# Mamba-2 part of a trunk kernel: channels on partitions, the group norm one stage later, the first output projections behind the last group's z columns

## The chip, the cores and the metric

The kernel runs on one core of a Trainium2 chip. The metric is the device time of one execution in microseconds: 1997.97 as the median of three (1996.41 to 1998.56). Profiles show one execution each. TensorE (PE) multiplies, VectorE (DVE), ScalarE (ACT) and GpSimd (POOL) do the rest, SyncE (SP) and POOL issue the DMAs. Each engine works through its own list in order; semaphores join the lists.

## What is computed

One layer of a decoder trunk on x of shape (1, 1024, 1024): a layer norm, a wide projection, a Conformer convolution branch beside a Mamba-2 branch, gates, an output projection, a second norm, a convolutional feed-forward block and a last norm. The change lies in the Mamba-2 branch (32 heads of 64 channels, four groups, state of 128, chunks of 128 positions):

```python
h = layer_norm(x, ln_in_g, ln_in_b)
u_glu, z, xbc, dt_raw, gate_a, gate_b = split_in(h @ w_in)
# in ssd_branch:
xbc = silu(causal_dwconv(xbc, conv_w, conv_b))           # xs, bm, cm
dt = softplus(dt_raw + dt_bias);  a = dt * -exp(a_log)
# in ssd_chunked, per chunk:
a_cs = cumsum(a)
y_diag = einsum("bcgrls,bcsgrp->bclgrp", cb * decay, xs * dt)
y_off  = einsum("bclgn,bcgrpn,bcgrl->bclgrp", cc, prev, exp(a_cs))
y = y_diag + y_off + xh * d_skip
yg = y * silu(z)                                          # groups of 512 channels
yg = yg * rsqrt(mean(square(yg), axis=-1) + RMS_EPS)      # per group and position
y_b = (yg * norm_w) @ w_ssm_out
mix = (sigmoid(gate_a) * y_a + sigmoid(gate_b) * y_b) @ w_o
```

## The kernel before

The 1024 positions go in two halves of 512 (`hh`). Activations stand channel-major in hT (128 channels on partitions, 512 positions along). fp32 products are made of three fp32r matmuls (`mm3`, L183 to L185: high by high, low by high, high by low); `project` (L187) makes one *column*, 128 output channels by 512 positions, of 24 matmuls 128x512. Its weights come by a DMA on SP, and `weights` splits them into high and low parts (cast on ACT L159, subtraction on DVE L160). Columns accumulate in four PSUM banks ("acc", `bank(1)`), everything else in four others ("sm", `bank(0)`).

`mixers` runs, per half, a stage for each of the four SSD groups: two columns for B and C (w_c), four for x, four for the gate z (`z_gate`, L478), two pairs for the Conformer part (`glu`: ga and gg), then `ssd_group` (L499) with its four chunks. Behind the groups come eight columns gt; then `combine` alternates gate columns (gb) with the second halves of the SSM output projection (sp). The first halves (so, `ssm_out_first`, which needs the normed groups 0 and 1) stand behind the SSD part of group 2. The 31-tap convolution (`conv31`, L467 on DVE) is recorded at low priority and fills VectorE's gaps.

In the SSD part positions stand on partitions. Per chunk, x is transposed (px), m = decay times CB is made, L562 computes po = C S (one matmul of 512 columns), L581 py (8 heads, m stationary, 64 columns of xs moving). VectorE puts t together: skip term (L551), yo (L564), t+yo (L567), t+py (L582), t times zs (L583); ACT squares it with a row sum into ssq (L585). zs comes from `z_gate` with positions on partitions as well. It has five buffers, and L583 is the last reader of each. `normed` then takes the root of four columns of ssq (L588, L589), scales the four t (L591) and transposes them into yT (16 transposes, L209, split into two parts at L215 and L216), where `so` and `sp` read them.

The order on each engine is fixed when the program is built: a simulated timeline chooses among ready instructions by priority. The pools' buffers decide who waits for whom.

Of the kernel before, what the change touches and what calls it, by code (L numbers as in the profile page):

```python
# [8 lines left out]
F32 = mybir.dt.float32  # L9
# [36 lines left out]
RW_NW = 6 * D  # L46
RW_AL = RW_NW + 2 * D
RW_SD = RW_AL + HEADS
RW_N = RW_SD + HEADS

# [6 lines left out]
def kernel(  # L57
# [71 lines left out]
    dskip = statep.tile([P, HEADS], F32, name="dskip")  # L129
# [8 lines left out]
    edc = statep.tile([P, 3, 4, HEADS], F32, name="edc")  # L138
# [12 lines left out]
    g_scr = [dram.tile([8, P, HALF], F32, name=f"g_scr{i}") for i in range(2)]  # L151
    y_scr = [dram.tile([8, P, HALF], F32, name=f"y_scr{i}") for i in range(2)]
# [111 lines left out]
    def ln_in(hh):  # L264
        hT = big_tile(f"hT{hh}")
        with pool(f"lnin{hh}", side="right") as pl:
# [12 lines left out]
            if first:  # L279
                SY.dma_start(pc[:, :PC_N], pcol)  # L280
                SY.dma_start(a_log, prow[RW_AL : RW_AL + HEADS].partition_broadcast(P))
                SY.dma_start(dskip, prow[RW_SD : RW_SD + HEADS].partition_broadcast(P))
# [12 lines left out]
    def time_steps(pl, hh, ps):  # L295

        n2 = 2 * HEADS
        dtc = pl.tile([n2, HALF], F32, tag="yo", name=f"dtc{hh}")
# [48 lines left out]
        for c in range(4):  # L347
# [6 lines left out]
            )  # L354
        hi = pl.tile([P, HALF], F32R, tag="xsd", name=f"sp_hi{hh}")
# [21 lines left out]
        A.activation(out=ev, in_=pe[:, : 3 * n], func=AF.Exp)  # L377
        V.tensor_mul(wds, dtv, edc[:, 1].rearrange("p c h -> p (c h)"))
# [99 lines left out]
    def z_gate(pl, hh, hT, g):  # L478

        pss = [bank(1) for _ in range(4)]  # L480
        for kp in range(4):
            w = weights(wz[g, kp], f"z{hh}_{g}_{kp}")
            for t in range(4):
                for k in range(2):
                    mm3(
                        pss[t],
                        lambda i: hT[:, i, 2 * kp + k, t * P : (t + 1) * P],
                        lambda i: w[:, i, k * HALF : (k + 1) * HALF],
                        kp == 0 and k == 0,
                        kp == 3 and k == 1,  # L490
                    )
        zs = []
        for t in range(4):
            z = pl.tile([P, HALF], F32, tag="zs", bufs=5, name=f"zs{hh}_{g}_{t}")
            A.activation(out=z, in_=pss[t], func=AF.Silu)
# [821 lines left out]
```

## Time and profile before

| | before |
|---|---|
| median of three runs | 1997.97 us |
| profiled execution | 1997.83 us, span 1995.9 us |
| mean granted TensorE clock | 0.998 |
| PE sum of matmuls L209 on t, L562, L581 | 15.3, 28.6, 60.5 us |
| DVE from 100 to 400 us | busy 298.40 of 300 us |
| DVE from 800 to 1050 us | busy 249.46 of 250 us |

The two stretches of VectorE are the mixers' group stages of the first and of the second half (TensorE is busy for 298.88 and 250.00 us in them). Busy times of overlapping matmuls are merged, and the mean of one record is its latency; what a stream of records costs is seen from the start of one to the start of the next.

### The profile page before, as it was taken

What the parts mean: (1) busy time and instruction counts of PE and PEld (TensorE: products, weight loads), DVE (VectorE), ACT (ScalarE), POOL (GpSimd) and SP (SyncE); (2) the same over time, 40 slices, a digit from 0 to 9 for tenths busy, and PEclk for the clock granted to TensorE, in tenths of its full rate; (3) what the DMA queues carried; (4) which work ended last, traced back from release to release, by engine and by line L of the source; (5) the groups of instructions that cost most, each with busy time, mean ns of one, the idle gap of its engine ahead of it and who ended that gap; (6) DMA issues with size and microseconds to landing.
All of it is one profiled execution on the core that took longest, in us unless ns stands there. A gap on an engine that the chain in (4) does not pass through costs nothing. (4 is left out here: it accounts for less than half of the span.)

```text
span 1995.9 us, 24560 instructions
## 1 busy us (share of the span) xinstructions
PE 1963.0 (98%) x9140; PEld 1619.0 (81%) x9140; DVE 1688.2 (85%) x2257; ACT 1025.6 (51%) x1490; POOL 170.2 (9%) x143
## 2 busy tenths in 40 slices
PE   7999999999999999999999999999999999999997
PEld 6888887888788888888888888887878888888886
DVE  7599999989865868999998987578998888788868
ACT  5465654556453265665545546255555544553432
POOL 1010101001310000100000122001000000011000
PEclk9999999999999999999999999999999999999999
DMA  6213223333445632222323243477443232368572
GB/s 223 95 64 96 80 89 107 96 111 102 168 136 164 229 124 74 85 90 85 116 90 111 101 166 125 137 277 250 154 155 110 100 122 95 106 225 270 181 242 106
DMA packets 97032, 272.21 MB, mean 136 GB/s; under 512 B 11216, under 2 KB 11216, under 8 KB 96912
## 3 DMA queue, kind: packets, MB, share of 16 engines
q1 hardware_dynamic: 88992, 246.78, 36.8%
q0 software_dynamic: 5616, 19.66, 2.7%
q10 hardware_dynamic: 2304, 4.20, 0.6%
q8 instruction: 72, 1.18, 0.2%
q14 instruction: 48, 0.39, 0.1%
HBM read 221.05 MB, written 49.55 MB: 136 GB/s over the span
## 5 line engine op out<-in xcount | busy, mean ns | idle before, releaser
L467 DVE SCALAR_TENSOR_TENSOR c<-v,pc,c 128x512 f32<-128x512 f32 x480 | 374.5, 803 | 7.1 <-ACT c L456 5.6
L525 POOL TENSOR_TENSOR au<-seg_mv,head_of 128x1024 fp32r<-128x1024 f32 x32 | 74.8, 2336 | 958.6 <-PE sm L534 728.7
L183 PE MATMUL acc<-hT,w_c 128*128 128x512 f32 x352 | 140.9, 400 | 0.0
L184 PE MATMUL acc<-hT,w_c 128*128 128x512 f32 x352 | 140.6, 399 | 0.0
L185 PE MATMUL acc<-hT,w_c 128*128 128x512 f32 x352 | 138.5, 394 | 0.0
L956 DVE SCALAR_TENSOR_TENSOR fo<-u,pc,fo 128x1024 f32<-128x1024 f32 x88 | 111.3, 1284 | 0.4 <-ACT fo L952 0.4
L422 DVE SCALAR_TENSOR_TENSOR xbc<-u,pc,xbc 128x512 f32<-128x512 f32 x144 | 109.6, 773 | 0.5 <-ACT xbc L420 0.4
L183 PE MATMUL acc<-h1s,w_s 128*128 128x512 f32 x264 | 103.4, 392 | 2.3 <-ACT u L940 2.3
L185 PE MATMUL acc<-h1s,w_s 128*128 128x512 f32 x264 | 103.0, 390 | 0.0
L184 PE MATMUL acc<-h1s,w_s 128*128 128x512 f32 x264 | 102.8, 389 | 0.0
L184 PE MATMUL acc<-w_z,hT 128*128 128x512 f32 x256 | 100.9, 394 | 0.0
L183 PE MATMUL acc<-w_z,hT 128*128 128x512 f32 x256 | 100.7, 400 | 0.0
L185 PE MATMUL acc<-w_z,hT 128*128 128x512 f32 x256 | 100.6, 396 | 0.0
L159 ACT CAST w_c<-st_c 128x1024 fp32r<-128x1024 f32 x48 | 50.4, 1051 | 91.8 <-PE acc L185 67.5
L1095 ACT CAST w_dn<-dr 128x1024 fp32r<-128x1024 f32 (+1 forms) x73 | 60.9, 843 | 67.9 <-DVE dr L1025 35.0
L1096 DVE TENSOR_TENSOR w_dn<-dr,w_dn 128x1024 fp32r<-128x1024 f32 (+1 forms) x73 | 70.2, 967 | 14.7 <-ACT w_dn L1095 14.5
L184 PEld LDWEIGHTS acc<-hT,w_c 128*128 128x128 f32 x352 | 66.1, 188 | 16.8 <-issue 3.9
L185 PEld LDWEIGHTS acc<-hT,w_c 128*128 128x128 f32 x352 | 66.1, 188 | 16.1 <-issue 2.6
L183 PEld LDWEIGHTS acc<-hT,w_c 128*128 128x128 f32 x352 | 66.1, 188 | 15.9 <-issue 2.6
L160 DVE TENSOR_TENSOR w_c<-st_c,w_c 128x1024 fp32r<-128x1024 f32 x46 | 59.3, 1288 | 16.7 <-ACT w_c L159 16.7
L183 PE MATMUL sm<-h1b,w_s 128*128 128x512 f32 x176 | 69.1, 393 | 0.0
L184 PE MATMUL sm<-h1b,w_s 128*128 128x512 f32 x176 | 69.0, 392 | 0.0
(366 smaller groups left out, 5698.0 us busy)
## 6 DMA issues: line engine op xcount, KB each, us to landing
st_c<-wcol SPq DMA_DIRECT2D x50, 512.0 KB, 3.5
st_z<-wz SPq DMA_DIRECT2D x32, 512.0 KB, 3.4
st_wo<-wo SPq DMA_DIRECT2D x24, 512.0 KB, 4.2
ra<-wup SPq DMA_DIRECT2D x22, 512.0 KB, 3.5
rb<-wup SPq DMA_DIRECT2D x22, 512.0 KB, 3.4
t_scr<-fo POOLq DMA_DIRECT2D x22, 512.0 KB, 3.4
dr<-t_scr SPq DMA_DIRECT2D x44, 256.0 KB, 4.0
dr<-wdown SPq DMA_DIRECT2D x38, 256.0 KB, 4.3
```

Of the source, the lines that this page charges most:

```text
L159: A.copy(w[:, 0, :], st)
L160: (eng or V).tensor_tensor(out=w[:, 1, :], in0=st, in1=w[:, 0, :].bitcast(F32), op=ALU.subtract)
L183: TE.matmul(ps, wa(0), xa(0), start=start, stop=False, skip_group_check=more)
L184: TE.matmul(ps, wa(0), xa(1), start=False, stop=False, skip_group_check=more)
L185: TE.matmul(ps, wa(1), xa(0), start=False, stop=stop, skip_group_check=more)
L422: V.scalar_tensor_tensor(out=o, in0=u[:, k : k + HALF], scalar=pc[:, wc + k : wc + k + 1], in1=o, op0=ALU.mult, op1=ALU.add,)
L467: V.scalar_tensor_tensor(out=accs[i], in0=v[:, k : k + HALF], scalar=pc[:, wc + k : wc + k + 1], in1=accs[i], op0=ALU.mult, op1=ALU.add,)
L525: G.tensor_tensor(out=au, in0=seg_mv[:, c, :].unsqueeze(1).to_broadcast([P, 8, P]), in1=head_of[:, g, :].unsqueeze(2).to_broadcast([P, 8, P]),
L956: V.scalar_tensor_tensor(out=o, in0=u[:, k : k + T], scalar=pc[:, wc + k : wc + k + 1], in1=o, op0=ALU.mult, op1=ALU.add,)
L1095: A.copy(w[:, 0, cs], src)
L1096: V.tensor_tensor(out=w[:, 1, cs], in0=src, in1=w[:, 0, cs].bitcast(F32), op=ALU.subtract)
```

## The change

z and y now stand with channels on partitions. `z_gate` makes four ordinary columns; one zs holds 128 channels by 512 positions. The exponentials of the cumulated decay, which scaled yo, are written to DRAM once per half (e_scr) and loaded by two broadcasting DMAs on POOL's queue into ys, which the group's four chunks then share (one buffer). A chunk multiplies its slice of ys by po (L564; po now four matmuls of 128 columns, L563) and adds py (L587; xs stationary with 64 columns, m moving with 128, heads alternately on the lower and the upper 64 partitions, L577). After the last chunk follow, per 128 channels, the skip term (L591), the multiplication by zs (L595), Square (L597, L600), and POOL sums the squares (L601). `normed` adds over partitions with four small matmuls (L606), takes the root (L611, L612), sends r to DRAM and back to all partitions (L614, L615), scales (L618) and splits (L203, L204). The transposes of t are gone, and the rows of norm_w too (nskip holds norm_w and D per channel). `done` of group g is called behind the z columns of group g+1, that of group 3 behind the second gt column; `ssm_out_first` behind the z columns of group 3.

```diff
-    dskip = statep.tile([P, HEADS], F32, name="dskip")
+    nskip = statep.tile([P, 2, 16], F32, name="nskip")
+    pick = statep.tile([P, 4, 4], F32, name="pick")
+    V.memset(pick, 0.0)
+    for c in range(4):
+        V.memset(pick[:, c, c : c + 1], 1.0)
...
+    e_scr = [dram.tile([P, HALF], F32, name=f"e_scr{i}") for i in range(2)]
+    r_scr = [dram.tile([GROUPS, HALF], F32, name=f"r_scr{i}") for i in range(2)]
...
+        eh = pl.tile([P, HALF], F32, tag="yo", bufs=2, name=f"sp_eh{hh}")
+        A.activation(out=eh, in_=pa, func=AF.Exp)
+        G.dma_start(e_scr[hh], eh)
...
-        for i, m in enumerate((upper, later, ones)):
+        for i, m in enumerate((later, ones)):
...
     def z_gate(pl, hh, hT, g):
 
-        pss = [bank(1) for _ in range(4)]
-        for kp in range(4):
-            w = weights(wz[g, kp], f"z{hh}_{g}_{kp}")
-            for t in range(4):
-                for k in range(2):
-                    mm3(
-                        pss[t],
-                        lambda i: hT[:, i, 2 * kp + k, t * P : (t + 1) * P],
-                        lambda i: w[:, i, k * HALF : (k + 1) * HALF],
-                        kp == 0 and k == 0,
-                        kp == 3 and k == 1,
-                    )
         zs = []
-        for t in range(4):
-            z = pl.tile([P, HALF], F32, tag="zs", bufs=5, name=f"zs{hh}_{g}_{t}")
-            A.activation(out=z, in_=pss[t], func=AF.Silu)
+        for i in range(4):
+            ps = bank(1)
+            project(ps, weights(wz[4 * g + i], f"z{hh}_{g}_{i}"), hT)
+            z = pl.tile([P, HALF], F32, tag="zs", bufs=5, name=f"zs{hh}_{g}_{i}")
+            A.activation(out=z, in_=ps, func=AF.Silu)
             zs.append(z)
         return zs
 
     def ssd_group(pl, hh, g, xT, BT, CT, zs):
         S = states[g]
         h8 = slice(8 * g, 8 * g + 8)
-        nw = row(pl, RW_NW + g * HALF, HALF, f"nw{hh}_{g}", tag="nw")
-        ssq = pl.tile([P, 4], F32, tag="ssq", name=f"ssq{hh}_{g}")
+        acc = pl.tile([P, 4, HALF], F32, tag="ys", name=f"ys{hh}_{g}")
+        ev = e_scr[hh].rearrange("(g k i j) t -> g k j i t", k=4, j=2, i=4)
+        for j in range(2):
+            G.dma_start(acc[j * HP : (j + 1) * HP], ev[g, 0, j].partition_broadcast(HP))
 
         def heads(t):
             return t.rearrange("p (h q) -> p h q", h=8)
@@ -508,7 +507,9 @@
         def per_head(t):
             return t.unsqueeze(2).to_broadcast([P, 8, HP])
 
-        ts = []
+        def by_tile(t):
+            return t.rearrange("p (i t) -> p i t", i=4)
+
         for c in range(4):
             nm = f"{hh}_{g}_{c}"
             cs = slice(c * P, (c + 1) * P)
@@ -547,8 +548,6 @@
             V.tensor_tensor(
                 out=heads(xs), in0=heads(px), in1=per_head(dts[0][:, c, h8]), op=ALU.mult
             )
-            t = pl.tile([P, HALF], F32, tag="t", bufs=5, name=f"t{nm}")
-            V.tensor_tensor(out=heads(t), in0=heads(px), in1=per_head(dskip[:, h8]), op=ALU.mult)
             if not last:
                 xsd = pl.tile([P, HALF], F32, tag="xsd", name=f"xsd{nm}")
                 V.tensor_tensor(
@@ -559,12 +558,10 @@
             V.tensor_tensor(out=m, in0=m, in1=cbm.unsqueeze(1).to_broadcast([P, 8, P]), op=ALU.mult)
             if not first:
                 po = bank(0)
-                TE.matmul(po, CT[:, cs], S, start=True, stop=True)
-                yo = pl.tile([P, HALF], F32, tag="yo", name=f"yo{nm}")
-                V.tensor_tensor(
-                    out=heads(yo), in0=heads(po), in1=per_head(edc[:, 0, c, h8]), op=ALU.mult
-                )
-                V.tensor_add(t, t, yo)
+                for i in range(4):
+                    ts = slice(i * P, (i + 1) * P)
+                    TE.matmul(po[:, ts], S[:, ts], CT[:, cs], start=True, stop=True)
+                V.tensor_tensor(out=acc[:, :, cs], in0=by_tile(po), in1=acc[:, :, cs], op=ALU.mult)
             if not last:
                 pn = bank(0)
                 TE.matmul(pn, bt, xsd, start=True, stop=True)
@@ -572,26 +569,57 @@
                     V.tensor_copy(S, pn)
                 else:
                     V.tensor_tensor(
-                        out=heads(S), in0=heads(S), in1=per_head(edc[:, 2, c, h8]), op=ALU.mult
+                        out=heads(S), in0=heads(S), in1=per_head(edc[:, 1, c, h8]), op=ALU.mult
                     )
                     V.tensor_add(S, S, pn)
             py = bank(0)
             for h in range(8):
-                hs = slice(h * HP, (h + 1) * HP)
-                TE.matmul(py[:, hs], m[:, h, :], xs[:, hs], start=True, stop=True)
-            V.tensor_add(t, t, py)
-            V.tensor_mul(t, t, zs[c])
-            sq = pl.tile([P, HALF], F32, tag="yo", name=f"sq{nm}")
-            A.activation(out=sq, in_=t, func=AF.Square, accum_out=ssq[:, c : c + 1])
-            ts.append(t)
+                TE.matmul(
+                    py[h % 2 * HP : (h % 2 + 1) * HP, h // 2 * P : (h // 2 + 1) * P],
+                    xs[:, h * HP : (h + 1) * HP],
+                    m[:, h, :],
+                    start=True,
+                    stop=True,
+                )
+            if first:
+                A.copy(acc[:, :, cs], by_tile(py))
+            else:
+                V.tensor_tensor(out=acc[:, :, cs], in0=acc[:, :, cs], in1=by_tile(py), op=ALU.add)
+        ss = pl.tile([P, HALF], F32, tag="ss", name=f"ss{hh}_{g}")
+        for i, y in enumerate(xT):
+            k = 4 * g + i
+            V.scalar_tensor_tensor(
+                out=y, in0=y, scalar=nskip[:, 1, k : k + 1], in1=acc[:, i, :],
+                op0=ALU.mult, op1=ALU.add,
+            )
+            V.tensor_mul(y, y, zs[i])
+            if i == 0:
+                A.activation(out=ss, in_=y, func=AF.Square)
+            else:
+                sq = pl.tile([P, HALF], F32, tag="yo", bufs=2, name=f"sq{hh}_{g}_{i}")
+                A.activation(out=sq, in_=y, func=AF.Square)
+                G.tensor_add(ss, ss, sq)
+
         def normed(yT):
-            A.activation(out=ssq, in_=ssq, func=AF.Sqrt, bias=eps, scale=1.0 / HALF)
-            V.reciprocal(out=ssq, in_=ssq)
+            pm = bank(0)
             for c in range(4):
+                TE.matmul(
+                    pm[:4, :P], pick[:, c, :], ss[:, c * P : (c + 1) * P],
+                    start=c == 0, stop=c == 3,
+                )
+            r = pl.tile([4, P], F32, tag="rr", name=f"rr{hh}_{g}")
+            A.activation(out=r, in_=pm[:4, :P], func=AF.Sqrt, bias=eps[:4], scale=1.0 / HALF)
+            V.reciprocal(out=r, in_=r)
+            rd = r_scr[hh][g]
+            G.dma_start(rd.rearrange("(c t) -> c t", c=4), r)
+            G.dma_start(ss, rd.partition_broadcast(P))
+            for i, y in enumerate(xT):
+                k = 4 * g + i
                 V.scalar_tensor_tensor(
-                    out=ts[c], in0=ts[c], scalar=ssq[:, c : c + 1], in1=nw, op0=ALU.mult, op1=ALU.mult
+                    out=y, in0=y, scalar=nskip[:, 0, k : k + 1], in1=ss,
+                    op0=ALU.mult, op1=ALU.mult,
                 )
-                transpose_to(yT, ts[c], c, (g % 2) * 4, 4)
+                split_to(yT, (g % 2) * 4 + i, y)
 
         return normed
...
                 zs = z_gate(pl, hh, hT, g)
+                if g == 3:
+                    ssm_out_first(pl, hh, yT)
+                if g % 2:
+                    yT = big_tile(f"yT{hh}_{g - 1}")
+                if g:
+                    done(yT)
                 vs = [(i, glu(pl, hh, hT, i)) for i in (2 * g, 2 * g + 1)]
                 done = ssd_group(pl, hh, g, xT, BT, CT, zs)
-                if g == 2:
-                    ssm_out_first(pl, hh, yT)
-                if g % 2 == 0:
-                    yT = big_tile(f"yT{hh}_{g}")
-                done(yT)
                 with tc.high_priority(offset=-1500):
...
+                if j == 1:
+                    done(yT)
```

The order of the instructions moves with it. First, TensorE in the second half at the end of group 1's SSD part, before: py of the last chunk (m_1_3) stands inside the column gg_4.

```order
L183 MATMUL acc_7662<-hT_5136,w_gg_4_7694 128x512
L184 MATMUL acc_7662<-hT_5136,w_gg_4_7694 128x512
L185 MATMUL acc_7662<-hT_5136,w_gg_4_7694 128x512
L183 MATMUL acc_7662<-hT_5136,w_gg_4_7694 128x512
L581 MATMUL sm_7186<-xs_1_3_7176,m_1_3_7165 128x64 x8
```

The same place of the change: it stands inside ga_4, seven records ahead of gg_4.

```order
L577 MATMUL sm_7138<-m_1_3_7118,xs_1_3_7129 64x128 x8
L189 MATMUL acc_7617<-hT_5108,w_ga_4_7621 128x512
L187 MATMUL acc_7617<-hT_5108,w_ga_4_7621 128x512
L188 MATMUL acc_7617<-hT_5108,w_ga_4_7621 128x512
L189 MATMUL acc_7617<-hT_5108,w_ga_4_7621 128x512
L187 MATMUL acc_7617<-hT_5108,w_ga_4_7621 128x512
L188 MATMUL acc_7617<-hT_5108,w_ga_4_7621 128x512
L189 MATMUL acc_7617<-hT_5108,w_ga_4_7621 128x512
L187 MATMUL acc_7618<-hT_5108,w_gg_4_7650 128x512
```

gg_4 accumulates in the bank that z_2_1, the second z column of the next group, held before it. What empties that bank stands in ScalarE's list; before, the first three of group 2's four Silus there (zs_2_0 to zs_2_2) stand among the third chunk's Square and the last chunk's Relu and Exp (m_1_3):

```order
L495 ACTIVATE zs_2_0_7653<-acc_7533 128x512
L585 ACTIVATE sq_1_2_7154,ssq_1_6999<-t_1_2_7127 128x512
L495 ACTIVATE zs_2_1_7655<-acc_7534 128x512
L542 ACTIVATE m_1_3_7165<-sm_7170 128x512
L543 ACT_TABLE_LOAD
L543 ACTIVATE m_1_3_7165<-m_1_3_7165 128x512
L495 ACT_TABLE_LOAD
L495 ACTIVATE zs_2_2_7657<-acc_7535 128x512
```

With the change, zs_2_1 stands behind the Square of group 1's first 128 channels (xbc_4 holds y by then):

```order
L163 CAST w_gg_5_7715<-st_gg_5_7713 128x1024
L597 ACTIVATE ss_1_7148<-xbc_4_6556 128x512
L492 ACT_TABLE_LOAD
L492 ACTIVATE zs_2_1_7529<-acc_7499 128x512
L600 ACTIVATE sq_1_1_7154<-xbc_5_6595 128x512
L492 ACTIVATE zs_2_2_7561<-acc_7531 128x512
```

And that Square follows the first L595 in VectorE's list, whose rows from py of the last chunk (sm_7138) on are now:

```order
L587 TENSOR_TENSOR ys_1_6962<-ys_1_6962,sm_7138 128x4x128
L474 SCALAR_TENSOR_TENSOR c_3_7169<-v_3_6957,pc,c_3_7169 128x512
L474 SCALAR_TENSOR_TENSOR c_2_7167<-v_2_6892,pc,c_2_7167 128x512
L591 SCALAR_TENSOR_TENSOR xbc_4_6556<-xbc_4_6556,nskip,ys_1_6962 128x512
L591 SCALAR_TENSOR_TENSOR xbc_5_6595<-xbc_5_6595,nskip,ys_1_6962 128x512
L591 SCALAR_TENSOR_TENSOR xbc_6_6634<-xbc_6_6634,nskip,ys_1_6962 128x512
L591 SCALAR_TENSOR_TENSOR xbc_7_6673<-xbc_7_6673,nskip,ys_1_6962 128x512
L474 SCALAR_TENSOR_TENSOR c_3_7169<-v_3_6957,pc,c_3_7169 128x512
L164 TENSOR_TENSOR w_gg_5_7715<-st_gg_5_7713,w_gg_5_7715 128x1024
L474 SCALAR_TENSOR_TENSOR c_2_7167<-v_2_6892,pc,c_2_7167 128x512
L595 TENSOR_TENSOR xbc_4_6556<-xbc_4_6556,zs_1_0_6711 128x512
```

(L474 is conv31, L164 the split of weights.) Before, L582 and L583 of the chunk stood there with two conv31 steps between them.

Last, TensorE at group 3's norm in the second half. Before, its sixteen transposes stand inside sp_0, behind that column's first records:

```order
L209 MATMUL sm_9055<-ident,t_3_0_8876 128x128 x4
L209 MATMUL sm_9063<-ident,t_3_1_8928 128x128 x4
L209 MATMUL sm_9071<-ident,t_3_2_8980 128x128 x4
L209 MATMUL sm_9079<-ident,t_3_3_9031 128x128 x4
L184 MATMUL acc_9487<-yT_2_8257,w_sp_0_9490 128x512
```

Now L606 stands between the end of gb_2 and the second half of sp_0, which reads group 3's part of yT:

```order
L187 MATMUL acc_9458<-hT_5108,w_gb_2_9461 128x512
L188 MATMUL acc_9458<-hT_5108,w_gb_2_9461 128x512
L189 MATMUL acc_9458<-hT_5108,w_gb_2_9461 128x512
L606 MATMUL sm_9134<-ss_3_8983,pick 4x128 x4
L187 MATMUL acc_9425<-yT_2_8644,w_sp_0_9428 128x512
```

In the first half seven records of gb_2 stand between L606 and sp_0.

More of the change, by code (lines that the diff above doesn't have):

```diff
@@ L137 @@
     dts = [statep.tile([P, 4, HEADS], F32, name=n) for n in ("dtv", "wds")]
-    edc = statep.tile([P, 3, 4, HEADS], F32, name="edc")
+    edc = statep.tile([P, 2, 4, HEADS], F32, name="edc")
     seg_mv = statep.tile([P, 4, P], F32, name="seg_mv")
@@ L279, in ln_in @@
             if first:
[L280 removed]
+                SY.dma_start(pc[:, :PC_N], pcol[:, :PC_N])
                 SY.dma_start(a_log, prow[RW_AL : RW_AL + HEADS].partition_broadcast(P))
[L282 removed]
+                SY.dma_start(nskip.rearrange("p i k -> p (i k)"), pcol[:, PC_N:])
             for t, xt in enumerate(xts):
@@ L297, in time_steps @@
         n2 = 2 * HEADS
-        dtc = pl.tile([n2, HALF], F32, tag="yo", name=f"dtc{hh}")
+        dtc = pl.tile([n2, HALF], F32, tag="yo", bufs=2, name=f"dtc{hh}")
         A.activation(
@@ L1286, in _pack @@
         "wcol": wcol,
-        "wz": rows(cz, GROUPS),
+        "wz": flat(cols(cz)),
         "wconv": flat(cols(a["w_conv_out"][0])),
```

14 lines of the change are left out of this document (6 added, 8 removed).

## The prediction

> **What bounds the kernel now.** I read the page's busy shares, its slices and chain, then the list of waits, and last the timelines of the places that the change touches.
>
> ```profile
> span 1995.9 us, 24560 instructions
> PE 1963.0 (98%) x9140; PEld 1619.0 (81%) x9140; DVE 1688.2 (85%) x2257; ACT 1025.6 (51%) x1490; POOL 170.2 (9%) x143
> PE   7999999999999999999999999999999999999997
> PE sm L209 <- DVE x L260: 13.3, 2, 12.1
> PE acc L184 <- DVE yT L216: 1.5, 1, 1.5
> PE acc L183 <- ACT gb L644: 0.6, 1, 0.6
> ```
>
> TensorE is the bound: 98% busy, nine tenths or more in all but the two outer slices. Its waits (total, times, longest) sum to some 22 us, of which 13.3 belong to the start. So two kinds of edit can move the time: those that alter the stream of matmuls, and those that make it wait. VectorE is 85% busy and works in a fixed order, so what TensorE newly waits for there comes late; a saving on VectorE alone gives nothing.
>
> **The change part by part.** The sum is made against the profiled execution, 1997.8 us (span 1995.9), which lies within 0.2 us of the median.
>
> *Matmuls.* The z columns keep 256 x 3 records of one shape. Three other parts differ:
>
> ```profile
> L209 PE MATMUL sm<-ident,t 128*128 128x128 f32 x128 | 15.3, 273 | 0.0
> L562 PE MATMUL sm<-state,xbc 128*128 128x512 f32 x56 | 28.6, 591 | 0.0
> L581 PE MATMUL sm<-xs,m 128*128 128x64 f32 x512 | 60.5, 271 | 0.0
> 516.36 1.91 PE L209 MATMUL sm<-ident,t 128*128 128x128 f32 x16
> 518.03 0.48 PE L183 MATMUL acc<-hT,w_gb 128*128 128x512 f32 x1
> 503.87 1.89 PE L581 MATMUL sm<-xs,m 128*128 128x64 f32 x16
> 505.57 0.48 PE L184 MATMUL acc<-hT,w_gb 128*128 128x512 f32 x1
> 476.26 1.02 PE L562 MATMUL sm<-state,xbc 128*128 128x512 f32 x2
> 476.71 0.79 PE L184 MATMUL acc<-hT,w_gt 128*128 128x512 f32 x1
> 499.79 0.39 PE L184 MATMUL acc<-hT,w_gb 128*128 128x512 f32 x1
> 500.02 0.39 PE L185 MATMUL acc<-hT,w_gb 128*128 128x512 f32 x1
> ```
>
> Records overlap, so I count from start to start. A projection record takes 0.23 us (499.79 to 500.02; 0.227 over longer stretches). The 16 transposes of one group (128 in eight blocks) hold TensorE for 1.67 us. L606 puts four small matmuls in their place, eight records at the transposes' 0.105 us and an estimated 0.2 around them: 1.04. That saves 0.63 in each of eight blocks, **-5.0**. L562's one matmul (two records, 0.45 us) becomes four of 128 columns, eight records, some 0.04 more by 28 blocks: +1.1. The third decay product dropped: -0.5.
>
> L577 is unknown: 64 columns stand still, 128 move, and outputs go alternately to the lower and upper 64 partitions. Now sixteen records take 1.70 us, 0.106 each, as long as the transposes' records of twice the moving columns; so the records' width doesn't price them. The nearest rows with a 64-wide stationary tile:
>
> ```profile
> 30.27 0.62 PE L394 MATMUL acc<-hT,w_c 128*64 128x256 f32 x4
> 30.72 1.24 PE L404 MATMUL acc<-hT,w_c 128*128 128x256 f32 x9
> 31.80 0.63 PE L394 MATMUL acc<-hT,w_c 128*64 128x256 f32 x4
> 704.74 0.39 PE L185 MATMUL acc<-hT,w_c 128*128 128x512 f32 x1
> 705.05 1.07 PE L304 MATMUL sm<-fold,dtc 64*128 64x32 f32 x8
> 706.06 0.50 PE L183 MATMUL acc<-hT,w_c 128*128 128x512 f32 x1
> ```
>
> Four 64-wide records take 0.45 us and nine full ones 1.08: no gain, and nothing lost on entering or leaving. L304, with 64 rows, begins 0.08 us late and holds 1.01 us for eight records, some 0.2 over their pitch. Taking nothing saved and nothing lost, as L394 shows, L577 stays at 1.7 us: **0**. Ends over 32 blocks: +0.3 each (L304's loss on entry and on exit), +10; or the two halves side by side at half of 1.70, less the same loss, -0.6 each, -19 (without the loss -27). The matmul side is thus -4.4, with ends -31 and +6.
>
> The Trainium skill, "TensorEngine Tiling (Array Packing)", section "When to Use Tiling", names this very swap (64 moving columns become stationary, two tiles) as up to twice as fast, and "Key Properties" has tiles work in parallel and a mode switch drain the array. By it the sum would be 19 lower; L304 agrees with a drain, L394 doesn't, and no row shows two tiles at once.
>
> *A new wait at the group boundary.* There are five zs buffers. Before, L583 freed one per chunk. Now L595 frees all four of a group after its last L577, so the next group's first column takes the fifth buffer and its second column's Silu (L492) waits for the first L595. ScalarE stands in order at the Square ahead of it (L597); behind it are queued the Silus of the third and fourth column and later casts. Three of the four accumulating banks stay full; one column (ga, or so_0) uses the fourth, and the next waits. TensorE's cover after the last L577, by the order shown above, in records of 0.227: 8+24 in the first half's group 0 (7.3 us), 23 in the second's (5.2); 11 and 7 for group 1 (2.5, 1.6); 11 and 9 for group 2 (2.5, 2.0).
>
> What must happen meanwhile, with pitches from VectorE's timeline:
>
> ```profile
> 278.57 1.89 PE L581 MATMUL sm<-xs,m 128*128 128x64 f32 x16
> 280.68 1.21 DVE L160 TENSOR_TENSOR w_gg<-st_gg,w_gg 128x1024 fp32r<-128x1024 f32 x1
> 281.81 1.41 DVE L467 SCALAR_TENSOR_TENSOR c<-v,pc,c 128x512 f32<-128x512 f32 x2
> 283.14 0.68 DVE L582 TENSOR_TENSOR t<-t,sm 128x512 f32<-128x512 f32 x1
> 292.10 2.73 DVE L591 SCALAR_TENSOR_TENSOR t<-t,ssq,nw 128x512 f32<-128x512 f32 x4
> L585 ACT ACTIVATE sq<-t 128x512 f32<-128x512 f32 x32 | 20.2, 631 | 19.7 <-DVE t L583 19.7
> L495 ACT ACTIVATE zs<-acc 128x512 f32<-128x512 f32 x32 | 18.4, 598 | 7.0 <-PE acc L185 6.9
> L495 ACT ACT_TABLE_LOAD x7 | 9.0, 1283 | 0.1
> ```
>
> L587 0.6, two conv31 steps 1.3, four L591 2.65, two more steps 1.3, a split 1.13, L595 0.7: 7.7 us. Then Square 0.63, table load 1.28, Silu 0.60, and 0.4 for hand-overs between engines: 10.6. VectorE also reaches L587 late: here L582 began 2.7 us after L581's end (280.46), and at the other seven group ends 1.9 to 5.8; since five steps per chunk become two, I take 2.0. So 12.6, less the cover: group 1 waits 10.1 and 11.0, group 2 10.1 and 10.6, group 0 4.0 (no table load stands there) and 6.3 (no split). In group 2 so_2 then waits again for a cast that needs so_1's end, with ya's copy, a Square and a Silu behind it (1.05+0.58+0.63+0.60+0.3): 3.2 in each half. **+58.5**; with no lateness 46, with 4 us 70. A single missing element doesn't remove it: the VectorE steps alone exceed every cover.
>
> *The last norm.* L606 of group 3 stands right ahead of the out-projection that needs it: 7 records between them in the first half, none in the second. The chain: sqrt 0.30, reciprocal 0.17, r to DRAM, its broadcast back, four L618 (as L591), cast and subtraction 0.7, hand-overs 0.5.
>
> ```profile
> nw<-prow SPq DMA_DIRECT2D x8, 256.0 KB, 3.3
> b_scr<-fo POOLq DMA_DIRECT2D x11, 256.0 KB, 2.3
> L674 POOL TENSOR_TENSOR mean<-mean,cc 128x512 f32<-128x512 f32 x12 | 18.5, 1540 | 2.3 <-DMA cc<-c_scr 1.5
> L588 ACT ACTIVATE ssq<-ssq,eps 128x4 f32<-128x4 f32 x8 | 2.4, 298 | 0.1
> ```
>
> With a write of 2.3 us on Pool's queue (2 KB may take less) and a broadcast of 3.3 it makes 9.9, less 1.6 of cover in the first half: 8.3 and 9.9. Today's 1.5 and 0.6 there go: **+16.1**. The two landings together may take 4 or 8 us: 12 to 21.
>
> *What costs nothing.* In groups 0 to 2, L606 stands 29 to 31 records (6.6 to 7.0 us) behind the end of the boundary wait, ahead of it three Squares and two Silus (3.1) and, partly beside them, Pool's three additions (1.5 each): tight, about 1 us over per group if they don't overlap. The rest of that norm has a stage of matmuls behind it. The ys loads (POOL, two of 512 KB per group, once L591 has emptied the buffer) and eh's Exp and write have several columns of 24 records (5.4 us) ahead of their first use. ssm_out_first keeps its matmuls, copies, weight loads and y_scr writes; on SP's queue they now stand behind the z weights of group 3, in the order in which TensorE uses them, and its cost is the so_2 wait above. The dropped nw rows were never waited for.
>
> *The clock.* After the 12.1 us wait at the start, records go at half pace:
>
> ```profile
> 12.11 3.65 PE L209 MATMUL sm<-ident,x 128*128 128x128 f32 x16 [12.11 <-DVE x L260]
> 16.98 1.94 PE L209 MATMUL sm<-ident,x 128*128 128x128 f32 x8 [1.23 <-DVE x L260]
> 19.58 1.05 PE L404 MATMUL acc<-hT,w_c 128*128 128x256 f32 x4
> 20.43 0.84 PE L394 MATMUL acc<-hT,w_c 128*64 128x256 f32 x3
> 21.28 0.70 PE L404 MATMUL acc<-hT,w_c 128*128 128x256 f32 x4
> ```
>
> Four L404 records end 1.05 us after the start at 19.58, and 0.70 after that at 21.28; from 16.98 on 4.3 us went at half pace, 2.1 lost. After the 1.5 us wait at L216 nothing slows. Eight new waits (six at boundaries, two at the norm) of 4 to 11 us lie between; most are nearer 12.1: **+17**, ends 0 and, if the first stretch counts too, 25.
>
> The Trainium skill, "TensorE: Matmul & The Clock Gate", Part 1, halves the clock after an idle window of about 3.4 us until as long a busy one; the start rows agree, and by it all eight pay 1.7, estimated 14.
>
> **Sum:** 1997.8 - 4.4 + 58.5 + 16.1 + 17 = 2085.0.
>
> **The rivals.** *A, halves side by side:* L577 at -19: 2066. For it: alternate outputs, sixteen independent records. Against: no row shows it. *B, shorter waits:* VectorE takes L587 at once (-12) and the clock holds (-17): 2056. For: VectorE loses three steps per chunk. Against: it was late in every quoted block. *C, dearer matmuls:* L577 +10, VectorE 4 us late (+11): 2106. *D, the other side, not slower:* the boundary is no wait at all, since VectorE's filler steps have run early and ScalarE frees the bank within the cover; then, with the halves side by side and the norm and its clock as counted (16 + 4), 1997.8 - 23 + 20 = 1995, or 1987 without the switching loss. It decides where the chain is shorter than the covers of 1.6 to 7.3 us instead of 12.6; L587, four L591 and L595 alone take 4. *E, the norm's delay hides nothing:* the waits on yT and gb that it could save are 2.1 in all, so this is no time of its own; it only takes the 2.1 from the sum (2087).
>
> **How the numbers follow.** Forecast (with E) 0.49, A 0.22, B 0.13, C 0.10, D 0.06, half of it at each of its times. The range runs from B with A's half of the gain, 2047, to C, 2108; it leaves out D and the tails. A measurement tells about 0.2%, 4 us. Faster 0.03, same 0.03, slower 0.94, since all cases but D end over 2040.
>
> **What would show it.** Right: TensorE's list of waits names L492 (Silu) at gg and so columns, six times 4 to 11 us, and L204/L618 at the second half of sp_0, twice 8 to 10; the projection records after each go at 0.43 us pitch for some 4 us. L577 at 1.7 us for sixteen records. Wrong: boundary waits under 3 us, L577 at 0.9, or a VectorE that reaches L587 with no lateness; the total falls below 2047 only if two of these hold.

## The result, and the profile after

The changed kernel takes 2067.59 us (median of four, 2065.33 to 2069.20) against 1997.19 for the kernel before: ratio 1.0354, 95% interval 1.0336 to 1.0372, 3.5% slower. The prediction said 2085 (2047 to 2108).

The page's head and TensorE's list of waits (engine, tile and line waiting, what released it: total us, times, longest):

```profile
span 2067.5 us, 24831 instructions
PE 1961.3 (95%) x9240; PEld 1603.2 (78%) x9240; DVE 1710.5 (83%) x2230; ACT 1040.9 (50%) x1474; POOL 240.7 (12%) x201
PE acc L187 <- ACT zs L492: 44.4, 6, 12.6
PE acc L187 <- ACT yT L203: 20.8, 2, 11.4
PE sm L213 <- DVE x L264: 13.5, 2, 12.2
PE sm L567 <- ACT bt L557: 5.8, 3, 2.4
PE acc L187 <- ACT ya L632: 3.2, 2, 1.6
...
PE acc L188 <- DVE yT L204: 2.3, 2, 1.1
PE sm L606 <- POOL ss L601: 1.9, 1, 1.9
```

TensorE is busy for as long as before (1961.3 us, 1963.0 before) in a span 71.6 us longer: the time went into waiting. All its waits sum to 96.6 us, 21.7 before: +74.9. A second part is in records that run at half pace. The timelines at the end of group 1's SSD part in the first half, on TensorE, VectorE and ScalarE:

```profile
294.58 0.80 PE L187 MATMUL acc<-hT,w_gg 128*128 128x512 f32 x1 [11.21 <-ACT zs L492]
295.17 0.63 PE L188 MATMUL acc<-hT,w_gg 128*128 128x512 f32 x1
295.60 0.63 PE L189 MATMUL acc<-hT,w_gg 128*128 128x512 f32 x1
...
298.09 0.40 PE L189 MATMUL acc<-hT,w_gg 128*128 128x512 f32 x1
298.32 0.39 PE L187 MATMUL acc<-hT,w_gg 128*128 128x512 f32 x1
```

```profile
284.25 0.67 DVE L587 TENSOR_TENSOR ys<-ys,sm 128x512 f32<-128x512 f32 x1
284.85 1.40 DVE L474 SCALAR_TENSOR_TENSOR c<-v,pc,c 128x512 f32<-128x512 f32 x2
286.18 2.73 DVE L591 SCALAR_TENSOR_TENSOR xbc<-xbc,nskip,ys 128x512 f32<-128x512 f32 x4
288.83 1.40 DVE L474 SCALAR_TENSOR_TENSOR c<-v,pc,c 128x512 f32<-128x512 f32 x2
290.15 1.21 DVE L164 TENSOR_TENSOR w_gg<-st_gg,w_gg 128x1024 fp32r<-128x1024 f32 x1
291.29 2.48 DVE L595 TENSOR_TENSOR xbc<-xbc,zs 128x512 f32<-128x512 f32 x4
```

```profile
292.00 0.63 ACT L597 ACTIVATE ss<-xbc 128x512 f32<-128x512 f32 x1 [7.55 <-DVE xbc L595]
292.63 1.28 ACT L492 ACT_TABLE_LOAD   x1
293.93 0.60 ACT L492 ACTIVATE zs<-acc 128x512 f32<-128x512 f32 x1
```

Read from the bottom, this is the chain the prediction described: the Silu that empties the bank starts at 293.93, behind a table load and the Square at 292.00, which waits for the first L595 (291.29), which stands behind L587 (284.25) and nine further VectorE steps. TensorE stands for 11.21 us. Then its records follow each other at 0.43 us (295.17 to 295.60) for 3.5 us and only from 298.09 on at 0.23; the granted clock reads 0.50 from 294 to 298 us and 1.00 from 298 to 300. Counted over the whole trace, 75 projection records have a start-to-start of 0.38 to 0.47 us, one before: +14.7 us. The remaining -18.0 us (71.6 - 74.9 - 14.7) is put down to the matmul side. Its main part is L577:

```profile
262.75 0.39 PE L187 MATMUL acc<-hT,w_z 128*128 128x512 f32 x1
263.07 1.09 PE L577 MATMUL sm<-m,xs 128*64 128x128 f32 x16
264.10 0.66 PE L520 MATMUL sm<-ident,xbc 128*128 128x128 f32 x4
```

In the kernel before, the record ahead of L581 (503.87):

```profile
503.64 0.39 PE L183 MATMUL acc<-hT,w_gb 128*128 128x512 f32 x1
```

Sixteen records take 1.03 us, where L581 took 1.70 (503.87 to 505.57): within the group, records for the lower and the upper half start 7 ns apart, and the next pair 0.10 later. From start to start the 512 records sum to 32.8 us, 55.1 before. A little of these 22.3 us goes on the way in and out. The record ahead of L577 holds TensorE for 0.32 us (262.75 to 263.07), that ahead of L581 for 0.23 (503.64 to 503.87), which is 2.5 us more in all blocks; the four L520 take 0.49, where the same four transposes took 0.44 before, some 1.6 us in all. That leaves about 18.

### The profile page after: what moved, and what is told of

Same layout as the page of the kernel before. It is cut to its first block, busy times and chain, and to the rows that moved or that the text cites. A ratio compares the mean times of both kernels' runs of the same rounds, so it can differ in the third digit from the quotient of the medians.

```text
span 2067.5 us, 24831 instructions
## 1 busy us (share of the span) xinstructions
PE 1961.3 (95%) x9240; PEld 1603.2 (78%) x9240; DVE 1710.5 (83%) x2230; ACT 1040.9 (50%) x1474; POOL 240.7 (12%) x201
## 4 chain that ended last, share of the span: by engine, by line
PE 58%; DVE 33%; issue 5%; DMA 3%; ACT 2%; SPq 0%; DVEq 0%; POOLq 0%; ACTq 0%
PE acc L187 15%; PE acc L188 15%; PE acc L189 15%; DVE c L474 13%; DVE xbc L429 3%; PE sm L187 3%; PE sm L188 3%; PE sm L189 3%; DVE m L558 1%; DVE w_c L164 1%; DMA ss<-r_scr 1%; DVE w_z L164 1%; PE acc L411 1%; DVE xbc L591 1%; DVE xbc L618 1%
## 5 line engine op out<-in xcount | busy, mean ns | idle before, releaser
L474 DVE SCALAR_TENSOR_TENSOR c<-v,pc,c 128x512 f32<-128x512 f32 x480 | 393.9, 845 | 6.2 <-ACT c L463 3.8
L526 POOL TENSOR_TENSOR au<-seg_mv,head_of 128x1024 fp32r<-128x1024 f32 x32 | 76.2, 2382 | 500.8 <-PE sm L535 500.7
L187 PE MATMUL acc<-hT,w_z 128*128 128x512 f32 x256 | 101.4, 396 | 0.0
L189 PE MATMUL acc<-hT,w_z 128*128 128x512 f32 x256 | 101.3, 396 | 0.0
L188 PE MATMUL acc<-hT,w_z 128*128 128x512 f32 x256 | 101.1, 395 | 0.0
L187 PE MATMUL acc<-hT,w_gg 128*128 128x512 f32 x128 | 53.7, 419 | 36.4 <-ACT zs L492 36.4
L189 PEld LDWEIGHTS acc<-hT,w_c 128*128 128x128 f32 x352 | 66.2, 188 | 16.1 <-issue 2.6
L164 DVE TENSOR_TENSOR w_c<-st_c,w_c 128x1024 fp32r<-128x1024 f32 x46 | 57.7, 1255 | 17.8 <-ACT w_c L163 17.8
L187 PE MATMUL acc<-yT,w_sp 128*128 128x512 f32 x128 | 52.3, 409 | 20.8 <-ACT yT L203 20.8
```

Of the source, the lines that this page charges most:

```text
L164: (eng or V).tensor_tensor(out=w[:, 1, :], in0=st, in1=w[:, 0, :].bitcast(F32), op=ALU.subtract)
L187: TE.matmul(ps, wa(0), xa(0), start=start, stop=False, skip_group_check=more)
L188: TE.matmul(ps, wa(0), xa(1), start=False, stop=False, skip_group_check=more)
L189: TE.matmul(ps, wa(1), xa(0), start=False, stop=stop, skip_group_check=more)
L474: V.scalar_tensor_tensor(out=accs[i], in0=v[:, k : k + HALF], scalar=pc[:, wc + k : wc + k + 1], in1=accs[i], op0=ALU.mult, op1=ALU.add,)
L526: G.tensor_tensor(out=au, in0=seg_mv[:, c, :].unsqueeze(1).to_broadcast([P, 8, P]), in1=head_of[:, g, :].unsqueeze(2).to_broadcast([P, 8, P]),
```

## The experiments

Each run is given with its edit to the changed kernel, unless it says otherwise, and with the kernel before on the same chip (1996 to 1997 us). Some runs that are compared with one another stood on different chips, so a difference of about 1 us between them says nothing.

**Is the wait one for zs buffers?** Two edits take it away in different ways. The first holds zs in bf16, so that nine buffers fit:

```diff
-            z = pl.tile([P, HALF], F32, tag="zs", bufs=5, name=f"zs{hh}_{g}_{i}")
+            z = pl.tile([P, HALF], mybir.dt.bfloat16, tag="zs", bufs=9, name=f"zs{hh}_{g}_{i}")
```

> The changed kernel with zs held in bf16, so that nine buffers fit where five did; the gate is thereby rounded to bf16 and the output differs by that. Theory (the wait at a group's end is for a free zs buffer): TensorE's waits on the Silu L492 fall from 44.4 us to under 3, with them the half-pace records behind them (about 9 of 14.9 us): 2014 us, 2008 to 2024. Rival 1 (ScalarE stands at the Square L597 whatever the buffers, or VectorE is simply too late): the waits stay over 20 us, or move to another row, 2045 or more.

Measured: 2018.33 us. No Silu wait is left in the list. The theory holds. The second keeps five buffers and moves the z columns back:

```diff
-                zs = z_gate(pl, hh, hT, g)
                 if g == 3:
                     ssm_out_first(pl, hh, yT)
...
                 vs = [(i, glu(pl, hh, hT, i)) for i in (2 * g, 2 * g + 1)]
+                zs = z_gate(pl, hh, hT, g)
```

> The changed kernel with z_gate called behind the Conformer columns (ga, gg) of its stage: the same five zs buffers, but the next group's second z column now comes 40 records or more after the last L577 of the group before. Theory: the Silu waits and the ya waits go (47.6 us) with about 9 us of half pace: 2011 us, 2004 to 2022. Rival 1: VectorE, 97% busy in these stages, is late elsewhere instead, and new waits of 20 us or more stand at other rows: 2030 to 2050.

Measured: 2009.12 us (2006.57 to 2010.28), 58 less than the changed kernel; the Silu and ya waits are gone and 4.3 of 14.9 us of half pace are left. The longest wait on yT fell too, from 11.4 to 6.8. Its list of waits begins, behind the start's, with what remains:

```profile
PE acc L187 <- ACT yT L203: 10.8, 2, 6.8
PE sm L567 <- ACT bt L557: 4.8, 2, 2.4
PE sm L535 <- ACT rr L611: 4.4, 2, 2.8
```

**What is L577's gain worth?** The eight heads in another order, alone, then with the z columns moved:

```diff
-            for h in range(8):
+            for h in (0, 2, 4, 6, 1, 3, 5, 7):
```

> The changed kernel with L577's eight heads in the order 0, 2, 4, 6, 1, 3, 5, 7, so that matmuls to the same half of the output partitions follow one another. Theory (the gain of L577, 1.03 us where L581 took 1.7, comes from two neighbours on different halves running at once): sixteen records take about 1.7 us again, 32 blocks by 0.67: plus 21, 2089 us, 2082 to 2095. Rival (a 64-wide stationary tile is by itself quicker): L577 stays at 1.03 and the time at 2067.

Measured: 2066.56 us, no change, and yet the theory on the records holds: L577's sum grew from 32.8 to 48.4 us. It isn't all of 55, since where the two runs of four meet some records still overlap: there they start 0.05 us apart, elsewhere in the group mostly 0.11.

```profile
261.43 1.58 PE L577 MATMUL sm<-m,xs 128*64 128x128 f32 x16
262.94 0.44 PE L520 MATMUL sm<-ident,xbc 128*128 128x128 f32 x2
```

TensorE's waits fell from 96.6 to 79.8 us, about as much as L577 grew: TensorE got to the same VectorE results later and waited less for them. So in the changed kernel 15.6 of the 22.3 us saved on L577 were worth nothing.

> z_gate behind the Conformer columns, and the heads in the order 0, 2, 4, 6, 1, 3, 5, 7 as in the run before that grouped them. There sixteen records of L577 grew from 32.8 to 48.4 us over all blocks and the time stayed, since the waits fell by as much. Theory (it stayed because the boundary waits took it up, and TensorE is the bound where they are gone): plus 12 to 16, 2021 to 2025 us. Rival (VectorE bounds the group stages, waits or not, and L577's gain is worth nothing in them): 2014 or less.

Measured with the z columns moved: 2013.49 us, 4.4 more, in the rival's range: even without boundary waits most of L577's gain is taken up by other waits (48.8 us in all without the grouping, 37.0 with it).

**Do the moved calls cost?** Norm and first output projections as in the kernel before, layout as changed:

```diff
-                if g == 3:
-                    ssm_out_first(pl, hh, yT)
-                if g % 2:
-                    yT = big_tile(f"yT{hh}_{g - 1}")
-                if g:
-                    done(yT)
...
                 done = ssd_group(pl, hh, g, xT, BT, CT, zs)
+                if g == 2:
+                    ssm_out_first(pl, hh, yT)
+                if g % 2 == 0:
+                    yT = big_tile(f"yT{hh}_{g}")
+                done(yT)
...
-                if j == 1:
-                    done(yT)
```

> The changed kernel with the norm called right behind its group's SSD part and the first output projections behind group 2's SSD part, as in the kernel before; the layout stays changed. Theory (the loss comes from the layout with its zs buffers, and from the last norm's chain, not from where norms and projections are called): the Silu waits stay near 44 us and the last norm's near 20, 2067 us, 2058 to 2076. Rival (the moves themselves cost): 2045 or less.

Measured: 2043.73 us, so the rival holds: the moves cost 24 us. Silu waits fell from 44.4 (6) to 36.4 (4), since group 2's two went; ya's 3.2 went; yT's fell from 20.8 to 15.7; half pace from 14.9 to 9.3. That is 21.9 of the 24 us. Which of the two moves costs more isn't told apart by this run.

**What is in the last norm's wait?** r to all partitions by TensorE, instead of to DRAM and back:

```diff
-            rd = r_scr[hh][g]
-            G.dma_start(rd.rearrange("(c t) -> c t", c=4), r)
-            G.dma_start(ss, rd.partition_broadcast(P))
+            pr = bank(0)
+            for c in range(4):
+                one = ident[:4, c : c + 1].to_broadcast([4, P])
+                TE.matmul(pr[:, c * P : (c + 1) * P], one, r, start=True, stop=True)
...
-                    out=y, in0=y, scalar=nskip[:, 0, k : k + 1], in1=ss,
+                    out=y, in0=y, scalar=nskip[:, 0, k : k + 1], in1=pr,
```

> The changed kernel with r brought to all partitions by four more small matmuls in each norm (r as the moving side, a row of ones as the stationary one) in place of the write to DRAM and the broadcasting load; L618 reads the bank. Theory (two thirds of the last norm's wait are those two transfers): from the issue of the write at 542.2 us to the start of L618 at 548.2 stand 6.0 us, the matmuls and a hand-over take about 1.3, so 4.7 us less in each half and with them some half pace: 2057 us, 2051 to 2061; the waits on yT fall from 23.1 to about 13. Rival (VectorE is late for the norm anyway, or the boundary waits take up what is saved): 2063 or more.

Measured: 2053.62 us, 14 less, as expected. The waits on yT fell from 23.1 to 7.8 us, further than to the 13 expected. Part of that is not the transfers: in the order built for this run 10 and 7 projection records stand between L606 and the first reader of the last yT (7 and 0 in the changed kernel), and the new matmuls themselves stand there too. With the z columns moved as well:

> Both mends: z_gate behind the Conformer columns, and r brought to all partitions by matmuls. Theory: of the 2009.1 us of the first mend alone the yT waits (14.2 us) fall to 4 or less, with 1 to 2 us of half pace: 1998 us, 1993 to 2003, about the kernel before. Rival 1 (VectorE, 97 to 99% busy in the group stages, bounds them and takes what TensorE gives up): 2004 or more. Rival 2 (the matmul side's savings now come through whole): 1990 or less.

Measured: 1994.20 us (1992.96 to 1996.18), ratio to the kernel before 0.9990 (0.9981 to 0.9999). The theory holds; these two mends make up the whole loss.

**What do POOL's additions cost?** With the z columns moved, first the additions left out, then kept but with a result that nothing reads:

```diff
-                G.tensor_add(ss, ss, sq)
+                G.tensor_add(sq, sq, sq)
```

> z_gate behind the Conformer columns, and the three additions L601 on POOL left out, so the norm counts a quarter of its squares (the output is not the reference's). Theory (VectorE is slowed while POOL works: L474's mean is 837 ns here, 803 in the kernel before, which has no such additions): L474's mean falls by 15 to 30 ns, VectorE's sum by some 10 us, and, with VectorE near the bound in the group stages, the time by 3 to 8 us, 2001 to 2006. Rival (the additions cost nothing): 2009 within 2.

> z_gate behind the Conformer columns, and the three POOL additions kept, but each into its own Square's tile, so that nothing waits for them (the norm counts a quarter of its squares, the output is not the reference's). The run without the additions was 31.5 us faster than that with them, where 3 to 8 were expected. Theory (their place in the norm's chain and in POOL's list is what costs, the slower VectorE less): L606 no longer waits for 6 us of additions, the yT waits go, but L474 stays near 837 ns and POOL's au (L526) still stands behind additions that wait for the Squares: 1988 us, 1983 to 1996. Rival 1 (VectorE's slowing is the cost): 2004 or more. Rival 2 (the chain is all): 1980 or less.

Measured: 1977.59 us without them, 1990.78 with them set aside, 2009.12 with them in place. The expectation of the first run missed by a factor of four: it had only VectorE's slowing in it. The second run's time is as its theory has it, not so the way that it gave. The timelines of POOL and TensorE in the run with the z columns moved and the additions in place, at the last norm of the first half of positions:

```profile
499.59 6.29 POOL L601 TENSOR_TENSOR ss<-ss,sq 128x512 f32<-128x512 f32 x3 [26.25 <-ACT sq L600]
511.65 0.54 POOL L614 DMA_DIRECT2D r_scr<-rr  x1 [5.78 <-DVE rr L612]
515.23 0.59 POOL L615 DMA_DIRECT2D ss<-r_scr  x1 [3.04 <-DMA r_scr<-rr]
```

```profile
508.95 1.04 PE L606 MATMUL sm<-ss,pick 128*4 128x128 f32 x8
520.07 0.80 PE L187 MATMUL acc<-yT,w_sp 128*128 128x512 f32 x1 [3.95 <-ACT yT L203]
```

The three additions take 6.29 us and end at 505.88, but L606 starts only at 508.95, without a wait before it: what holds it is its place in TensorE's list, behind ten records of sp_0. Between L606 and the first reader of the last yT stand 26 records here and 12 in the second half of positions. With the additions set aside 52 stand there in both, 66 records or 15 us more of cover (an estimate at 0.227 each), and the yT waits go (14.2 to 0.2 us). So the 18.3 us go with another place of L606 in the order, and hardly with the time that the additions took on the chip; a run that changes that place alone wasn't made. Both edits also free the norm of three of its four Squares, and what that is worth isn't told apart. Left out altogether, the additions give another 13.2 us. VectorE's conv31 in the two runs, set aside first:

```profile
L474 DVE SCALAR_TENSOR_TENSOR c<-v,pc,c 128x512 f32<-128x512 f32 x480 | 383.4, 829 | 5.5 <-ACT c L463 4.1
```

```profile
L474 DVE SCALAR_TENSOR_TENSOR c<-v,pc,c 128x512 f32<-128x512 f32 x480 | 370.5, 802 | 6.4 <-ACT c L463 4.9
```

The same 480 steps take 12.9 us less. That POOL's work slows VectorE is shown: with the additions set aside, the 15 steps that overlap one of them take 1.43 us on average, and the 418 that overlap no work of POOL take 0.74, as they do in the run without (435 steps, 0.74). How much of the 13.2 us comes by that way, and how much by POOL's own list (L526 stands behind L601), is not shown.

**A version that beats both.** z columns moved; the squares summed by TensorE over partitions and channels at once, root and reciprocal on ScalarE:

```diff
+        pm = bank(0)
...
-                G.tensor_add(ss, ss, sq)
...
+            TE.matmul(pm, ones, sq, start=i == 0, stop=i == 3)
+        A.activation(out=ss, in_=pm, func=AF.Ln, bias=eps, scale=1.0 / HALF)
+        A.activation(out=ss, in_=ss, func=AF.Exp, scale=-0.5)
...
-            G.dma_start(ss, rd.partition_broadcast(P))
```

> z_gate behind the Conformer columns; the squares are summed by four accumulating matmuls with a matrix of ones right behind the SSD part, which leaves the sum on all partitions, and ScalarE makes the root's reciprocal with Ln and Exp: no POOL additions, no VectorE reciprocal, no transfers. Theory: like the run without POOL additions (1977.6 us), plus 8 x (1.8 - 1.0) us for the larger sums: 1984 us, 1977 to 1989, faster than both kernels; no wait on yT. Rival (ScalarE's extra table loads and the held bank make new waits): 1992 or more.

Measured: 1991.21 us (1989.57 to 1992.88), ratio 0.9971 (0.9960 to 0.9982): no wait on yT, TensorE's waits 22.8 us in all, but 7 us slower than expected. The sums cost more than 1.8 us:

```profile
181.93 1.02 PE L594 MATMUL sm<-sq,ones 128*128 128x512 f32 x2
182.39 0.80 PE L183 MATMUL acc<-hT,w_z 128*128 128x512 f32 x1
183.02 1.02 PE L594 MATMUL sm<-sq,ones 128*128 128x512 f32 x2
```

From one sum to the next go 1.09 us, one projection record (0.23) among them: 0.86 for two fp32 records of 512 columns. The timeline had given them 0.45, since the second half of the price shows in the record behind. So the heads were grouped here too, and then each sum made a single record:

> The run before this one with the heads in the order 0, 2, 4, 6, 1, 3, 5, 7. L577 grew by 15.6 us when so grouped; the time grew by 0 in the changed kernel and by 4.4 with the boundary waits gone. Theory (a saving of TensorE's counts in full where TensorE waits for nothing): plus 12 to 16 us over the run before. Rival (VectorE bounds the group stages all the same): plus 5 or less.

Measured: 2003.82 us, 12.6 more. Here, where TensorE waits for almost nothing, most of L577's 15.6 us count: the theory holds. The next edit is against the run with the sums on TensorE, without the grouping:

```diff
+    ones_r = statep.tile([P, P], F32R, name="ones_r")
+    V.tensor_copy(ones_r, ones)
...
-            sq = pl.tile([P, HALF], F32, tag="yo", bufs=2, name=f"sq{hh}_{g}_{i}")
+            sq = pl.tile([P, HALF], F32R, tag="yo", bufs=2, name=f"sq{hh}_{g}_{i}")
...
-            TE.matmul(pm, ones, sq, start=i == 0, stop=i == 3)
+            TE.matmul(pm, ones_r, sq, start=i == 0, stop=i == 3)
```

> As the run with the sums on TensorE, with the squares and the matrix of ones in fp32r, so that each sum is one pass over TensorE (the squares are rounded to fp32r before they are added). Theory (TensorE is the bound now, and what it is spared comes through): 32 records of 0.227 us in place of 64 of about 0.247 are 8.5 us less: 1983 us, 1980 to 1986. Rival (VectorE bounds the group stages): 1988 or more.

Measured: 1973.80 us (1971.81 to 1974.37), ratio 0.9887 (0.9869 to 0.9904): 1.1% faster than the kernel before. It gained 17.4 us, not 8.5, as the price of a sum was 0.86 us: 32 x (0.86 - 0.23) would be 20.

## Why the prediction was right, step by step

The time lay 17.4 us under the forecast and 1.6 over rival A. The mechanism, TensorE waiting at the group boundaries and at the last norm and then running at half pace, was right; several sizes were not. The two runs that remove the boundary waits and the two that shorten the last norm's chain show it.

| term | forecast | measured |
|---|---|---|
| matmul side (what the other rows leave) | -4.4 | -18.0 |
| boundary waits (Silu, ya) | +58.5 | +47.6 |
| last norm (yT), less 2.1 | +16.1 | +21.0 |
| half pace | +17 | +14.7 |
| bt, L606 and other waits | 0 | +6.3 |

- **L577** is a term that failed: "nothing saved and nothing lost, as L394 shows". Its records saved 22.3 us, about 18 with the loss on entering and leaving. L394's records all went to one half of the partitions, so they could not show the overlap of two; the row was near in shape and silent on the point. Rival A had it, at -19. By the run with grouped heads at least 15.6 of it was worth nothing in this kernel: what L577 no longer takes shows again among the waits.
- **Rival A's time** was met by luck. With the heads grouped the matmul side comes to -4.1 us, near the forecast's -4.4, and the time is still 18 us under the forecast. There the boundary waits are 39.2 us, where 58.5 were forecast: 29.9 of 31.4 for groups 0 and 1, 9.3 of 27.1 for group 2. So the forecast lay high by group 2's boundary, and not by L577. The terms of the sum weren't independent either: a longer matmul side shortened the waits.
- **L562 to L563**: the +1.1 was about right, but not by its working as printed, which gave two records 0.45 us. The row behind them (476.71 to 477.35) holds the rest, 0.86 in all. The eight records of L563 take 0.81, and the record behind them loses 0.09 too. Counted so, the 28 blocks took 24.1 us before and 25.0 after.
- **Boundary**: groups 0 and 1 cost 36.4 us (4.57, 8.05, 11.21, 12.55), forecast 31.4. The steps from L587 to the first L595 took 7.0 us at five of the six ends, as forecast, but VectorE reached L587 later than the 2.0 us assumed: 3.1 to 4.3 us behind the last L577's end, 3.7 on average, close to rival C's 4. At group 2's end in the first half it was 3.1 (L577 ended at 389.31, L587 began at 392.44):

```profile
388.22 1.09 PE L577 MATMUL sm<-m,xs 128*64 128x128 f32 x16
389.24 0.50 PE L188 MATMUL acc<-yT,w_so 128*128 128x512 f32 x1
393.65 0.50 PE L187 MATMUL acc<-yT,w_so 128*128 128x512 f32 x1 [1.62 <-ACT ya L632]
402.76 0.50 PE L187 MATMUL acc<-yT,w_so 128*128 128x512 f32 x1 [3.38 <-ACT zs L492]
```

```profile
392.44 0.67 DVE L587 TENSOR_TENSOR ys<-ys,sm 128x512 f32<-128x512 f32 x1
```

  Group 2 was forecast at 27.1 and cost 11.2 (3.38 and 4.61 for the Silu, 1.62 twice for ya). The step that failed is the cover: so_1 waited only for ya's copy of so_0 (1.62) and so could run its 24 records before so_2 met the full bank (3.38). The prediction had so_1 meet it.
- **Last norm**: forecast 9.9 us without cover, measured 11.41 in the second half of positions, where no record stands between L606 and its reader:

```profile
1241.71 1.04 PE L606 MATMUL sm<-ss,pick 128*4 128x128 f32 x8
1242.79 1.28 ACT L611 ACT_TABLE_LOAD   x1
1244.08 0.36 ACT L611 ACTIVATE rr<-sm,eps 4x128 f32<-4x128 f32 x1
1244.83 0.93 DVE L612 RECIPROCAL rr<-rr 4x128 f32<-4x128 f32 x1
1246.06 0.54 POOL L614 DMA_DIRECT2D r_scr<-rr  x1 [4.41 <-DVE rr L612]
1249.03 0.59 POOL L615 DMA_DIRECT2D ss<-r_scr  x1 [2.43 <-DMA r_scr<-rr]
1252.70 2.74 DVE L618 SCALAR_TENSOR_TENSOR xbc<-xbc,nskip,ss 128x512 f32<-128x512 f32 x4 [6.93 <-DMA ss<-r_scr]
1254.15 0.79 PE L187 MATMUL acc<-yT,w_sp 128*128 128x512 f32 x1 [11.41 <-ACT yT L203]
```

  A table load of 1.28 us ahead of the root was put at nothing. The reciprocal took 0.93 us where 0.17 was taken (four rows of 128 elements, not 128 rows of four), and write and broadcast 6.6 (1246.06 to 1252.70) where 5.6 were taken. Against that, only the first of the four L618 stands before TensorE starts again, where all four (2.65) were counted (a second wait of 1.15 us, for the subtraction, follows). In the first half the table load ran ahead of L606 (534.33), but the reciprocal began 2.05 us behind the root's end, at 540.92, as VectorE was still in conv31. POOL's additions were called tight, about 1 us over per group if they don't overlap; in the changed kernel one wait of 1.9 us shows them.
- **Half pace**: right for this kernel. It follows its waits from 3.38 us on, and none of the shorter ones, up to 2.4 us. The Trainium skill, "TensorE: Matmul & The Clock Gate", Part 1, has an idle window of about 3.4 us; the changed kernel's rows agree with it, but other runs don't: half pace followed a wait of 2.77 us with the z columns moved (at 972.13 us) and one of 1.94 with the additions set aside (at 449.84). So no run here fixes from which wait on it comes. At the start of the kernel before, where the price of 2.1 us was taken, the granted clock reads 1.00 from 12 to 24 us, and behind the new waits 0.50; that the two are the same thing isn't shown.
- **Rival B** and **rival D** fell with the waits and the half pace as measured. **Rival E**, the norm's delay as no time of its own, isn't confirmed: the delayed norm and the moved projections together cost 24 us, of which 11.2 are waits at the projections (group 2's Silu 8.0, ya 3.2) and 5.1 the last norm's wait on yT; the run that undid both moves doesn't part them.

## What to carry to other kernels

When a layout makes one result the last reader of a whole group of buffers, count what the next group needs before that reader has run: five buffers served a reader per chunk, and the same five stopped TensorE six times once the reader came at the end. A saving on TensorE counts only at places where it waits for nothing: the same 15.6 us were worth 0, 4.4 and 12.6 us as the waits were taken away. Additions given to an idle engine aren't free: VectorE steps that overlapped them took 1.43 us instead of 0.74, and with them the small matmuls that need their sum stood later in TensorE's list, with 26 and 12 records of cover instead of 52.

## What the runs showed of the hardware

Two 64-wide stationary tiles whose outputs go to different halves of the partitions run side by side: pairs start 7 ns apart and sixteen records take 1.03 us instead of 1.70. Entering isn't free: the record ahead of the group takes 0.32 us instead of 0.23. The Trainium skill, "TensorEngine Tiling (Array Packing)", section "Key Properties", says that tiles work in parallel; the trace agrees, and grouping the heads by half, which took the sixteen records to 1.51 us, bears it out. An fp32 record of 512 moving columns takes 0.43 us, an fp32r one 0.23, and as an fp32 matmul shows as two such records, a timeline that is read by the start of the group and of the next one leaves half of the price in the record that follows.
